# Later transposes and attention pairs, pooling sums on VectorE, and features-first values in a one-core decoder layer

## The chip, the cores and the metric

The kernel runs on one NeuronCore of a Trainium2 chip. The metric is the device time of one launch in microseconds (us). Five engines work from queues of their own, each in program order: TensorE (PE, with PEld for its weight loads) multiplies matrices into PSUM; VectorE (DVE), ScalarE (ACT) and GpSimd (POOL) do elementwise work; SyncE (SP) issues the transfers. GpSimd is used here on SBUF only. Semaphores order the engines.

## The reference

One hybrid decoder layer on 256 tokens of 1024 features, all in float32:

```
proj = rmsnorm(x) @ w_in                  # q, k, v (512 each), u_pool 512, gates 2048
q, k = rotary(rmsnorm_per_head(q, k))     # 8 heads of 64
attn = causal softmax(q k^T / 8) v        # one block of 256 tokens, so plain causal attention
pool = (trailing mean over 2, 4, 8, 16 tokens - token) @ w_pool, scaled
g = sigmoid(gates + b)
x = x + (g0 * (attn @ w_branch_attn) + g1 * (pool @ w_branch_pool)) @ w_out
up = depthwise_conv3(rmsnorm(x) @ w_up);  gate, val = split(up)
out = x + (silu(gate) * val) @ w_down     # 2816 hidden features
```

With 256 tokens and blocks of 256, block selection selects nothing beyond the own block.

## The kernel before

Activations are kept features-first (128 features on partitions, 256 tokens along the free axis), except q, k and v, which are computed tokens-first, 128 tokens at a time. Precision comes from splitting: each operand of a large product is split into a rounded `high` part (ScalarE, L78) and the rest `low` (VectorE, L82 or L84), and `mm3` (L90 to L92) adds three products. Weights are streamed in chunks of 1 MB into four `raw` buffers; `ahead` splits the next piece (half a chunk, `hi_...` on ScalarE, `lo_...` on VectorE) some pieces before TensorE needs it, and the last `low` of a chunk issues the next load on SyncE's queue.

Every engine's work is in the order in which the Python program writes it; the last lines of the kernel tie each instruction to the one before it on its engine. So the order around the change is that of the code:

- `project` computes q, k, v. While k and v run, `norm_evacuate` (L281) normalises and rotates q and k, mostly on GpSimd (L294 to L305).
- `to_heads` (L308) transposes a normalised half of q or k with four TensorE transposes and copies it on ScalarE to `qT` or `kT` (L313).
- Four feature tiles of the pooling projection follow (two chunks `p`, two tiles each, 24 matmuls a tile). `pool_group` (L380) takes each tile, and sums shifted copies in 1 to 4 doubling steps on GpSimd; `pool_mean` comes two tiles later.
- Sixteen gate tiles follow (`ps_g`, 24 matmuls each). Four attention pairs (two heads each) are woven between them: `scores` (L422) at the gate tiles 0, 4, 8, 12, and then, through `later(n, ...)` and `tick`, which is called once per tile, `weigh` three tiles later (transposes of the weights), `values` one later, `heads_out` one later. At tile 10 `pool_maps` multiplies by `w_pool`.
- `branch` then computes the pooling branch (`ps_bp`, 8 tiles of 12 matmuls; `tick` at every second tile) and the attention branch (`ps_ba`), which needs the heads' outputs `ath` and `atl`. After that come the output projection and the ConvFFN, which the diff does not touch.

PSUM is shared: a pool of four banks (`bank`) serves the projections, the transposes and the values; a second pool with two buffers of two banks (`ps2`) serves scores, transposed weights and the pool maps. A tile that reuses a buffer waits for the last reader of the tile before.

Of the kernel before, what the change touches and what calls it, by code (L numbers as in the profile page):

```python
# [20 lines left out]
DH = 64  # L21
# [10 lines left out]
NEG = -1e30  # L32
# [18 lines left out]
STAGGER = 1  # L51
AHEAD = 4
FFN_AHEAD = 6
XCUTS = (1, 2, 4, 6, 8)


@with_exitstack
def hybrid_layer_kernel(ctx: ExitStack, tc: tile.TileContext, xq_d, par_d, wkv_d, wpg_d,
                        wpool_d, wba_d, wbp_d, wout_d, wup_d, wdn_d, out_d):
    nc = tc.nc  # L60
# [10 lines left out]
    tmp = mixer.enter_context(tc.tile_pool(name="tmp", bufs=2))  # L71

    def bank(name):
        return mm.tile([P, 512], F32, tag="mm", name=name)


    def high(hi, src, scale=1.0):
        nc.scalar.activation(hi, src, AF.Copy, scale=scale)  # L78

    def low(lo, hi, src, scale=None):  # L80
        if scale is None:
            nc.vector.tensor_tensor(lo, src, hi.bitcast(F32), ALU.subtract)  # L82
        else:
            nc.vector.scalar_tensor_tensor(lo, src, scale, hi.bitcast(F32), ALU.mult, ALU.subtract)  # L84
# [41 lines left out]
    for c, (name, src) in enumerate(order):  # L126
        n = CH if name == "q" else src.shape[-1]
# [31 lines left out]
    def ahead(upto=0):  # L159

        next_high()
        next_low()
        if at[1] - sum(p[0] < used[0] for p in pieces) < upto:
            next_high()
            next_low()
# [23 lines left out]
    cut = 0  # L189
    for k in XCUTS:  # L190
        end = KD + k * (S + AW)
# [9 lines left out]
    for i in range(WARM):  # L201
        nc.tensor.matmul(warm[:, 0:P], ones, ones, start=True, stop=True)

    ident = const.tile([P, P], F32, name="ident")
# [2 lines left out]
    nc.gpsimd.memset(mhalf, -0.5)  # L207
    mask = const.tile([P, 3, P], F32, name="mask")
    nc.gpsimd.memset(mask, 0.0)
    nc.gpsimd.affine_select(out=mask[:, 1:3, :], in_=mask[:, 1:3, :], compare_op=ALU.is_ge, fill=NEG,  # L210
                            base=0, pattern=[[0, 2], [-1, P]], channel_multiplier=1)
    rcnt = const.tile([P, 16], F32, name="rcnt")
    nc.gpsimd.iota(rcnt, pattern=[[1, 16]], base=1, channel_multiplier=0,
# [38 lines left out]
    qT, kT = qkT[:, 0], qkT[:, 1]  # L252
    vn = act.tile([P, 2 * NT, AW], F32, tag="v", name="vn")
# [54 lines left out]
    def to_heads(qg, t, dst, name):  # L308
        pq = bank(f"ps_t{name}{t}")
        flat = qg.rearrange("p h d -> p (h d)")  # L310
        for j in range(KA):
            nc.tensor.transpose(pq[:, j * P:(j + 1) * P], flat[:, j * P:(j + 1) * P], ident)
        nc.scalar.activation(dst[:, :, t * P:(t + 1) * P], pq.rearrange("p (j c) -> p j c", c=P), AF.Copy)  # L313
# [32 lines left out]
    qg, kg, stat = [], [], []  # L346
# [2 lines left out]
    ptv = project("v", on_v)  # L349
    for t in range(NT):  # L350
        nc.scalar.activation(vn[:, t, :], ptv[t], AF.Copy, scale=rtok1[:, t:t + 1])
    for t in range(NT):
        to_heads(qg[t], t, qT, "q")


    due = {}
    clock = [0]
# [1 line left out]
    def later(n, fn, *args):  # L359
        due.setdefault(clock[0] + n, []).append((fn, args))  # L360
# [7 lines left out]
    def feature_tile(w, c, name):  # L368
        hi, lo = w
        ps = bank(f"ps_{name}")  # L370
        for k in range(KD):
            sl = slice(k * 256 + c * P, k * 256 + (c + 1) * P)
            mm3(ps[:, 0:S], (hi[:, sl], lo[:, sl]), (xhi[:, k, :], xlo[:, k, :]), k == 0, k == KD - 1)
        return ps
# [3 lines left out]
    PAD = 16  # L378

    def pool_group(g, ps):  # L380
        w = WINDOWS[g]
        u = tmp.tile([P, PAD + S], F32, tag="pu", name=f"pu{g}")
        nc.gpsimd.memset(u[:, 0:PAD], 0.0)
        nc.vector.tensor_tensor(u[:, PAD:], ps[:, 0:S], R1, ALU.mult)
        cur, step = u, 1
        while step < w:
            nxt = tmp.tile([P, PAD + S], F32, tag=f"pw{step % 3}", bufs=2, name=f"pw{g}_{step}")
            nc.gpsimd.tensor_copy(nxt[:, 0:step], cur[:, 0:step])
            nc.gpsimd.tensor_tensor(nxt[:, step:], cur[:, step:], cur[:, 0:PAD + S - step], ALU.add)
            cur, step = nxt, 2 * step  # L390
        later(2, pool_mean, g, u, cur)

# [10 lines left out]
    for b in range(2):  # L403
        w = chunk("p")
        for c in range(2):
            ps = feature_tile(w, c, f"u{b}{c}")
            tick()
            ahead()
            pool_group(2 * b + c, ps)
    for t in range(NT):  # L410
        to_heads(kg[t], t, kT, "k")


    ath = act.tile([P, KA, S], F32R, tag="ath", name="ath")
    atl = act.tile([P, KA, S], F32R, tag="atl", name="atl")
    gates = xq[:, :, S:].rearrange("p k (i s) -> p k i s", s=S)

    def gate(n):
        return gates[:, n // 2, n % 2, :]

    def scores(hp):
        ps = ps2.tile([P, 2, 512], F32, tag="ps2", name=f"ps_s{hp}")  # L422
        for j in range(2):
            rows = slice(j * DH, (j + 1) * DH)
            nc.tensor.matmul(ps[:, j, 0:S], qT[rows, hp, P:S], kT[rows, hp, :], start=True, stop=True)
            nc.tensor.matmul(ps[:, j, S:S + P], qT[rows, hp, 0:P], kT[rows, hp, 0:P], start=True, stop=True)
        sm = tmp.tile([P, 2, 3 * P], F32, tag="big", bufs=4, name=f"sm{hp}")
        nc.vector.tensor_tensor(sm, ps[:, :, 0:3 * P],
                                mask.rearrange("p a b -> p (a b)")[:, None, :].to_broadcast([P, 2, 3 * P]), ALU.add)
        mx = tmp.tile([P, 2, 2], F32, tag="mx", name=f"mx{hp}")  # L430
        nc.vector.tensor_reduce(mx[:, 1, :], sm[:, :, 0:S], axis=AX.X, op=ALU.max)
        nc.vector.tensor_reduce(mx[:, 0, :], sm[:, :, S:3 * P], axis=AX.X, op=ALU.max)
        nc.vector.tensor_scalar(mx, mx, -(DH ** -0.5), None, op0=ALU.mult)
        sums = tmp.tile([P, 2, 2], F32, tag="sums", name=f"sums{hp}")
        for j in range(2):
            for t, cols in ((1, slice(0, S)), (0, slice(S, 3 * P))):
                nc.scalar.activation(sm[:, j, cols], sm[:, j, cols], AF.Exp, bias=mx[:, t, j:j + 1],
                                     scale=DH ** -0.5, accum_out=sums[:, t, j:j + 1])
        later(3, weigh, hp, sm, sums)

    def weigh(hp, sm, sums):
        pp = ps2.tile([P, 2, 512], F32, tag="ps2", name=f"ps_p{hp}")
        for j in range(2):
            for b in range(3):
                nc.tensor.transpose(pp[:, j, b * P:(b + 1) * P], sm[:, j, b * P:(b + 1) * P], ident)
        rs = tmp.tile([P, 2, 2], F32, tag="rs", name=f"rs{hp}")
        nc.vector.reciprocal(rs, sums)
        pT = tmp.tile([P, 2, 3 * P], F32, tag="big", bufs=4, name=f"pT{hp}")
        nc.scalar.activation(pT, pp[:, :, 0:3 * P], AF.Copy)
        later(1, values, hp, pT, rs)  # L450

    def values(hp, pT, rs):
        po = bank(f"ps_o{hp}")
        pov = po[:, 0:2 * P].rearrange("p (t j d) -> p t j d", t=2, j=2)
        for j in range(2):
            h = 2 * hp + j
            cs = slice(h * DH, (h + 1) * DH)
            nc.tensor.matmul(pov[:, 0, j, :], pT[:, j, S:3 * P], vn[:, 0, cs], start=True, stop=True)
            nc.tensor.matmul(pov[:, 1, j, :], pT[:, j, 0:P], vn[:, 0, cs], start=True, stop=False)
            nc.tensor.matmul(pov[:, 1, j, :], pT[:, j, P:S], vn[:, 1, cs], start=False, stop=True)  # L460
        an = tmp.tile([P, 2, 2, DH], F32, tag="an", name=f"an{hp}")
        nc.vector.tensor_tensor(an, pov, rs[:, :, :, None].to_broadcast([P, 2, 2, DH]), ALU.mult)
        later(1, heads_out, hp, an)

    def heads_out(hp, an):
        pa = bank(f"ps_a{hp}")
        for t in range(NT):
            nc.tensor.transpose(pa[:, t * P:(t + 1) * P], an[:, t].rearrange("p j d -> p (j d)"), ident)
        high(ath[:, hp, :], pa[:, 0:S])
        low(atl[:, hp, :], ath[:, hp, :], pa[:, 0:S])  # L470

    waiting = list(range(KD, 2 * KD)) + list(range(KD))

# [21 lines left out]
            low(pooll[:, g, :], poolh[:, g, :], o, par[:, C_PS + g:C_PS + g + 1])  # L495

    for n in range(2 * KD):
        if n % 4 == 0:
            scores(n // 4)
        if n == 10:  # L500
            pool_maps()
            ahead()
        b, c = n // 2, n % 2
        if c == 0:
            w = chunk("g")
        ps = feature_tile(w, c, f"g{n}")
        tick()
        ahead(AHEAD if n % 2 else 0)
        nc.vector.tensor_tensor(gate(n), ps[:, 0:S], R1, ALU.mult)
        if n >= 2 * KD - 2:  # L510
            sigmoids(3)
# [22 lines left out]
    tmp = ctx.enter_context(tc.tile_pool(name="ffn", bufs=2))  # L534
# [122 lines left out]
    ps = [bank("ps_up1_0")]  # L657
# [8 lines left out]
    for i in range(1, KF):  # L666
        if i > 1:
            w = chunk("up")
            ps = [up_tile(w, 0, i)]
# [8 lines left out]
        if i >= LAG:  # L678
# [92 lines left out]
```

## Time and profile before

| | |
|---|---|
| time, median of 3 runs | 358.66 us (357.54 to 359.63) |
| time of the profiled execution | 356.89 us |
| its span on the core | 355.1 us |
| mean granted TensorE clock | 0.995 |
| busy: PE, DVE, ACT, POOL | 344.3, 255.3, 195.4, 101.7 us |

The profile is of one execution. L with a number is a line of the kernel. A group's row gives line, engine, operation, output <- inputs, shapes and count, then busy time and mean, then the engine's idle time just before and what ended it. In a timeline a row starts with the start and the duration in us; several equal instructions in sequence are merged (x4). Matmuls overlap in TensorE's pipeline, so the spacing of their starts, not their duration, is what one costs. A two-pass float32 matmul is two instructions.

### The profile page before, as it was taken

The numbers are of one execution on the slowest core, as the hardware profiler recorded it, in microseconds if no ns is written. First come the engines' busy times: TensorE is split into PE (matmuls) and PEld (weight loads), VectorE is DVE, ScalarE is ACT, GpSimd is POOL, SyncE is SP. The second block draws the span as 40 slices with busy tenths as digits, with TensorE's granted clock in tenths as the row PEclk, the third lists the DMA queues.
The fourth block names the chain that finished last, engine by engine and source line by source line (L and its number), as shares of the span: only waits on it lengthen the run. The fifth ranks groups of instructions, "written<-read, shape, count | busy, mean of one in ns | idle before, by whom it ended". The sixth has DMA issues, their size and how long they took to land.

```text
span 355.1 us, 6775 instructions
## 1 busy us (share of the span) xinstructions
PE 344.3 (97%) x2760; PEld 334.5 (94%) x2760; DVE 255.3 (72%) x401; ACT 195.4 (55%) x311; POOL 101.7 (29%) x127
## 2 busy tenths in 40 slices
PE   8999895999999999999999999999999999999996
PEld 6887794999999999999999999999999999999996
DVE  4879727944677597499789986667777777777743
ACT  5955614636464984566467565555555555556420
POOL 1008999100000006379232222121212121212140
PEclk9999998999999999999999999999999999999999
DMA  7985623244263464075534764646455453642003
GB/s 281 420 341 178 252 90 119 49 173 170 116 236 120 173 258 163 6 293 194 221 117 140 278 236 180 220 145 231 134 222 185 172 228 128 238 132 107 2 0 118
DMA packets 10254, 62.76 MB, mean 177 GB/s; under 512 B 1136, under 2 KB 2288, under 8 KB 3312
## 3 DMA queue, kind: packets, MB, share of 16 engines
q1 hardware_dynamic: 10224, 62.34, 48.3%
q8 instruction: 21, 0.34, 0.4%
q14 instruction: 9, 0.07, 0.1%
HBM read 61.29 MB, written 1.05 MB: 176 GB/s over the span
## 4 chain that ended last, share of the span: by engine, by line
PE 75%; POOL 8%; DVE 8%; DMA 3%; ACT 2%; issue 2%; SPq 1%; POOLq 0%
PE ps_up L91 11%; PE ps_up L90 11%; PE ps_up L92 11%; PE ps_d L633 6%; PE ps_d L632 6%; PE ps_d L634 6%; PE ps_g L90 5%; PE ps_g L91 4%; PE ps_g L92 4%; DMA raw_k<-in_wkv 3%; DVE lo_up L82 2%; DVE hlo L84 2%; POOL rh_k L294 1%; POOL rh_q L294 1%; PE ps_bp L90 1%
## 5 line engine op out<-in xcount | busy, mean ns | idle before, releaser
L91 PE MATMUL ps_up<-hlo,hi_up 128*128 128x256 f32 x352 | 98.5, 280 | 0.2 <-DVE hlo L84 0.2
L90 PE MATMUL ps_up<-hhi,hi_up 128*128 128x256 f32 x352 | 98.7, 280 | 0.0
L92 PE MATMUL ps_up<-hhi,lo_up 128*128 128x256 f32 x352 | 98.4, 280 | 0.0
L91 PEld LDWEIGHTS ps_up<-hlo,hi_up 128*128 128x128 f32 x352 | 66.2, 188 | 0.4 <-DVE hlo L84 0.4
L90 PEld LDWEIGHTS ps_up<-hhi,hi_up 128*128 128x128 f32 x352 | 66.2, 188 | 0.0
L92 PEld LDWEIGHTS ps_up<-hhi,lo_up 128*128 128x128 f32 x352 | 66.2, 188 | 0.0
L82 DVE TENSOR_TENSOR lo_up<-raw_up,hi_up 128x1024 fp32r<-128x1024 f32 x44 | 55.9, 1274 | 6.1 <-ACT hi_up L78 6.1
L615 POOL TENSOR_TENSOR c_v<-c_g,c_v 128x256 f32<-128x256 f32 x22 | 16.3, 740 | 120.7 <-DVE c_v L598 120.7
L633 PE MATMUL ps_d<-al,hi_dn 128*128 128x256 f32 x176 | 49.2, 280 | 0.0
L634 PE MATMUL ps_d<-ah,lo_dn 128*128 128x256 f32 x176 | 49.2, 280 | 0.0
L632 PE MATMUL ps_d<-ah,hi_dn 128*128 128x256 f32 x176 | 49.2, 279 | 0.0
L78 ACT ACTIVATE hi_up<-raw_up 128x1024 fp32r<-128x1024 f32 x44 | 44.9, 1045 | 0.0
L90 PE MATMUL ps_g<-xhi,hi_g 128*128 128x256 f32 x128 | 37.5, 293 | 0.0
L91 PE MATMUL ps_g<-xlo,hi_g 128*128 128x256 f32 x128 | 36.3, 284 | 0.0
L92 PE MATMUL ps_g<-xhi,lo_g 128*128 128x256 f32 x128 | 36.3, 284 | 0.0
L78 ACT ACTIVATE ah<-c_v 128x256 fp32r<-128x256 f32 x22 | 9.2, 418 | 45.9 <-POOL c_v L615 45.9
L634 PEld LDWEIGHTS ps_d<-ah,lo_dn 128*128 128x128 f32 x176 | 33.1, 188 | 0.0
L632 PEld LDWEIGHTS ps_d<-ah,hi_dn 128*128 128x128 f32 x176 | 33.1, 188 | 0.0
L633 PEld LDWEIGHTS ps_d<-al,hi_dn 128*128 128x128 f32 x176 | 33.1, 188 | 0.0
L545 POOL TENSOR_TENSOR xq<-xq 128x256 f32<-128x256 f32 x8 | 7.0, 887 | 74.1 <-issue 70.1
L82 DVE TENSOR_TENSOR lo_dn<-raw_dn,hi_dn 128x1024 fp32r<-128x1024 f32 x22 | 27.8, 1265 | 0.4 <-ACT hi_dn L78 0.4
L603 DVE TENSOR_TENSOR u_v<-ps_up,R 128x256 f32<-128x256 f32 x22 | 9.3, 422 | 26.1 <-PE ps_up L92 26.1
(191 smaller groups left out, 843.7 us busy)
## 6 DMA issues: line engine op xcount, KB each, us to landing
raw_up<-in_wup SPq DMA_DIRECT2D x22, 1024.0 KB, 4.8
raw_dn<-in_wdn SPq DMA_DIRECT2D x11, 1024.0 KB, 4.8
raw_g<-in_wpg SPq DMA_DIRECT2D x8, 1024.0 KB, 4.8
raw_o<-in_wout SPq DMA_DIRECT2D x4, 1024.0 KB, 4.8
xq<-in_xq SPq DMA_DIRECT2D x3, 768.0 KB, 7.3
raw_v<-in_wkv SPq DMA_DIRECT2D x2, 1024.0 KB, 14.0
raw_p<-in_wpg SPq DMA_DIRECT2D x2, 1024.0 KB, 6.3
raw_bp<-in_wbp SPq DMA_DIRECT2D x2, 1024.0 KB, 5.5
```

Of the source, the lines that this page charges most:

```text
L78: nc.scalar.activation(hi, src, AF.Copy, scale=scale)
L82: nc.vector.tensor_tensor(lo, src, hi.bitcast(F32), ALU.subtract)
L84: nc.vector.scalar_tensor_tensor(lo, src, scale, hi.bitcast(F32), ALU.mult, ALU.subtract)
L90: nc.tensor.matmul(out, sh, mh, start=start, stop=False, **kw)
L91: nc.tensor.matmul(out, sh, ml, start=False, stop=False, **kw)
L92: nc.tensor.matmul(out, sl, mh, start=False, stop=stop, **kw)
L294: nc.gpsimd.tensor_tensor(rh, ss, mhalf[:, 0:H], ALU.pow)
L603: nc.vector.tensor_tensor(u, ps[:, 0:S], R2, ALU.mult)
L615: nc.gpsimd.tensor_tensor(uc[1], g[1], uc[1], ALU.mult)
L632: nc.tensor.matmul(o, hi[:, sl], acch[i], start=first, stop=False, skip_group_check=True)
L633: nc.tensor.matmul(o, hi[:, sl], accl[i], start=False, stop=False, skip_group_check=True)
L634: nc.tensor.matmul(o, lo[:, sl], acch[i], start=False, stop=i == KF - 1, skip_group_check=True)
```

## The change

1. `to_heads` for q moves from before the pooling tiles to after the first two of them; `to_heads` for k moves from after the pooling tiles to just before gate tile 1 (`KREADY`).
2. `scores` runs at gate tiles 2, 6, 10, 14 (`FIRST`) instead of 0, 4, 8, 12, and `weigh` four tiles after it instead of three.
3. The doubling sums of `pool_group` run on VectorE, and without the copies of the first columns: each step starts at column 2·step − 1, since only columns from 16 − w on are ever read. The memset of the padding moves to VectorE as well.
4. The softmax weights are divided by their sums before they are transposed: the reciprocal directly follows the exponentials, and two GpSimd products per pair multiply the weights. `values` then multiplies with v as the stationary operand, so that the output is features-first; each head writes one half of the partitions. The division after the values, the two transposes and `heads_out` go; `high` and `low` read the values' PSUM bank directly.
5. The three 128-column blocks of a pair's scores are reordered (tokens 0 to 127 first), and the mask with them.

```diff
+KREADY = 1
+FIRST = 2
...
-    nc.gpsimd.affine_select(out=mask[:, 1:3, :], in_=mask[:, 1:3, :], compare_op=ALU.is_ge, fill=NEG,
+    nc.gpsimd.affine_select(out=mask[:, 0:3:2, :], in_=mask[:, 0:3:2, :], compare_op=ALU.is_ge, fill=NEG,
...
-    for t in range(NT):
-        to_heads(qg[t], t, qT, "q")
...
-        nc.gpsimd.memset(u[:, 0:PAD], 0.0)
+        nc.vector.memset(u[:, 0:PAD], 0.0)
...
-            nc.gpsimd.tensor_copy(nxt[:, 0:step], cur[:, 0:step])
-            nc.gpsimd.tensor_tensor(nxt[:, step:], cur[:, step:], cur[:, 0:PAD + S - step], ALU.add)
+            a = 2 * step - 1
+            nc.vector.tensor_tensor(nxt[:, a:], cur[:, a:], cur[:, a - step:PAD + S - step], ALU.add)
...
             pool_group(2 * b + c, ps)
-    for t in range(NT):
-        to_heads(kg[t], t, kT, "k")
+        if b == 0:
+            for t in range(NT):
+                to_heads(qg[t], t, qT, "q")
...
+    TOK = (slice(0, P), slice(P, 3 * P))
...
-            nc.tensor.matmul(ps[:, j, 0:S], qT[rows, hp, P:S], kT[rows, hp, :], start=True, stop=True)
-            nc.tensor.matmul(ps[:, j, S:S + P], qT[rows, hp, 0:P], kT[rows, hp, 0:P], start=True, stop=True)
+            nc.tensor.matmul(ps[:, j, P:3 * P], qT[rows, hp, P:S], kT[rows, hp, :], start=True, stop=True)
+            nc.tensor.matmul(ps[:, j, 0:P], qT[rows, hp, 0:P], kT[rows, hp, 0:P], start=True, stop=True)
...
-        later(3, weigh, hp, sm, sums)
+        rs = tmp.tile([P, 2, 2], F32, tag="rs", name=f"rs{hp}")
+        nc.vector.reciprocal(rs, sums)
+        for t in (1, 0):
+            n = TOK[t].stop - TOK[t].start
+            nc.gpsimd.tensor_tensor(sm[:, :, TOK[t]], sm[:, :, TOK[t]],
+                                    rs[:, t, :, None].to_broadcast([P, 2, n]), ALU.mult)
+        later(4, weigh, hp, sm)
...
-        later(1, values, hp, pT, rs)
-
-    def values(hp, pT, rs):
+        later(1, values, hp, pT)
+
+    def values(hp, pT):
+
         po = bank(f"ps_o{hp}")
-        pov = po[:, 0:2 * P].rearrange("p (t j d) -> p t j d", t=2, j=2)
-        for j in range(2):
-            h = 2 * hp + j
-            cs = slice(h * DH, (h + 1) * DH)
-            nc.tensor.matmul(pov[:, 0, j, :], pT[:, j, S:3 * P], vn[:, 0, cs], start=True, stop=True)
-            nc.tensor.matmul(pov[:, 1, j, :], pT[:, j, 0:P], vn[:, 0, cs], start=True, stop=False)
-            nc.tensor.matmul(pov[:, 1, j, :], pT[:, j, P:S], vn[:, 1, cs], start=False, stop=True)
-        an = tmp.tile([P, 2, 2, DH], F32, tag="an", name=f"an{hp}")
-        nc.vector.tensor_tensor(an, pov, rs[:, :, :, None].to_broadcast([P, 2, 2, DH]), ALU.mult)
-        later(1, heads_out, hp, an)
-
-    def heads_out(hp, an):
-        pa = bank(f"ps_a{hp}")
-        for t in range(NT):
-            nc.tensor.transpose(pa[:, t * P:(t + 1) * P], an[:, t].rearrange("p j d -> p (j d)"), ident)
-        high(ath[:, hp, :], pa[:, 0:S])
-        low(atl[:, hp, :], ath[:, hp, :], pa[:, 0:S])
+        for b in range(2):
+            for j in range(2):
+                h = 2 * hp + j
+                nc.tensor.matmul(po[j * DH:(j + 1) * DH, b * P:S], vn[:, b, h * DH:(h + 1) * DH],
+                                 pT[:, j, 2 * b * P:(2 * b + 2 - b) * P], start=b == 0, stop=b == 1)
+        high(ath[:, hp, :], po[:, 0:S])
+        low(atl[:, hp, :], ath[:, hp, :], po[:, 0:S])
...
     for n in range(2 * KD):
-        if n % 4 == 0:
-            scores(n // 4)
+        if n == KREADY:
+            for t in range(NT):
+                to_heads(kg[t], t, kT, "k")
+        if n >= FIRST and (n - FIRST) % 4 == 0:
+            scores((n - FIRST) // 4)
```

More of the change, by code (lines that the diff above doesn't have):

```diff
@@ L430, in scores @@
         mx = tmp.tile([P, 2, 2], F32, tag="mx", name=f"mx{hp}")
-        nc.vector.tensor_reduce(mx[:, 1, :], sm[:, :, 0:S], axis=AX.X, op=ALU.max)
-        nc.vector.tensor_reduce(mx[:, 0, :], sm[:, :, S:3 * P], axis=AX.X, op=ALU.max)
+        for t in (1, 0):
+            nc.vector.tensor_reduce(mx[:, t, :], sm[:, :, TOK[t]], axis=AX.X, op=ALU.max)
         nc.vector.tensor_scalar(mx, mx, -(DH ** -0.5), None, op0=ALU.mult)
@@ L435, in scores, with weigh @@
         for j in range(2):
-            for t, cols in ((1, slice(0, S)), (0, slice(S, 3 * P))):
-                nc.scalar.activation(sm[:, j, cols], sm[:, j, cols], AF.Exp, bias=mx[:, t, j:j + 1],
+            for t in (1, 0):
+                nc.scalar.activation(sm[:, j, TOK[t]], sm[:, j, TOK[t]], AF.Exp, bias=mx[:, t, j:j + 1],
                                      scale=DH ** -0.5, accum_out=sums[:, t, j:j + 1])
-        later(3, weigh, hp, sm, sums)
-    def weigh(hp, sm, sums):
+        rs = tmp.tile([P, 2, 2], F32, tag="rs", name=f"rs{hp}")
+        nc.vector.reciprocal(rs, sums)
+        for t in (1, 0):
+            n = TOK[t].stop - TOK[t].start
+            nc.gpsimd.tensor_tensor(sm[:, :, TOK[t]], sm[:, :, TOK[t]],
+                                    rs[:, t, :, None].to_broadcast([P, 2, n]), ALU.mult)
+        later(4, weigh, hp, sm)
+    def weigh(hp, sm):
         pp = ps2.tile([P, 2, 512], F32, tag="ps2", name=f"ps_p{hp}")
@@ L445, in weigh @@
                 nc.tensor.transpose(pp[:, j, b * P:(b + 1) * P], sm[:, j, b * P:(b + 1) * P], ident)
-        rs = tmp.tile([P, 2, 2], F32, tag="rs", name=f"rs{hp}")
-        nc.vector.reciprocal(rs, sums)
         pT = tmp.tile([P, 2, 3 * P], F32, tag="big", bufs=4, name=f"pT{hp}")
         nc.scalar.activation(pT, pp[:, :, 0:3 * P], AF.Copy)
-        later(1, values, hp, pT, rs)
-    def values(hp, pT, rs):
+        later(1, values, hp, pT)
+    def values(hp, pT):
         po = bank(f"ps_o{hp}")
-        pov = po[:, 0:2 * P].rearrange("p (t j d) -> p t j d", t=2, j=2)
-        for j in range(2):
-            h = 2 * hp + j
-            cs = slice(h * DH, (h + 1) * DH)
-            nc.tensor.matmul(pov[:, 0, j, :], pT[:, j, S:3 * P], vn[:, 0, cs], start=True, stop=True)
-            nc.tensor.matmul(pov[:, 1, j, :], pT[:, j, 0:P], vn[:, 0, cs], start=True, stop=False)
-            nc.tensor.matmul(pov[:, 1, j, :], pT[:, j, P:S], vn[:, 1, cs], start=False, stop=True)
-        an = tmp.tile([P, 2, 2, DH], F32, tag="an", name=f"an{hp}")
-        nc.vector.tensor_tensor(an, pov, rs[:, :, :, None].to_broadcast([P, 2, 2, DH]), ALU.mult)
-        later(1, heads_out, hp, an)
-    def heads_out(hp, an):
-        pa = bank(f"ps_a{hp}")
-        for t in range(NT):
-            nc.tensor.transpose(pa[:, t * P:(t + 1) * P], an[:, t].rearrange("p j d -> p (j d)"), ident)
-        high(ath[:, hp, :], pa[:, 0:S])
-        low(atl[:, hp, :], ath[:, hp, :], pa[:, 0:S])
+        for b in range(2):
[5 more added lines that the diff above has]
+        low(atl[:, hp, :], ath[:, hp, :], po[:, 0:S])
     waiting = list(range(KD, 2 * KD)) + list(range(KD))
```

## The prediction

> **What bounds the kernel now.** I read the page's head, then TensorE's waits, the chain of waits, the timeline around the longest wait, and the stage tables.
>
> ```profile
> span 355.1 us, 6775 instructions
> ...
> PE 344.3 (97%) x2760; PEld 334.5 (94%) x2760; DVE 255.3 (72%) x401; ACT 195.4 (55%) x311; POOL 101.7 (29%) x127
> ```
>
> TensorE is busy nearly throughout, so only two things can help: filling its holes, or giving it less to do. Its waits, longest first (total, times, longest):
>
> ```profile
> PE ps_s L425 <- ACT qkT L313: 4.1, 1, 4.1
> ...
> PE ps_tq L312 <- POOL qg_q L305: 1.0, 1, 1.0
> ```
>
> The two waits with attention's names are what the change aims at. The chain of waits (start, duration, what) shows what lies behind the long one:
>
> ```profile
> 51.64 0.47 POOL qg_k L305
> 52.41 0.59 POOL pw L389
> ...
> 56.45 0.56 DVE pl L399
> 57.45 0.95 ACT hi_g L78
> 58.40 0.98 ACT qkT L313 x2
> 59.42 0.73 PE ps_s L425 x4
> ```
>
> GpSimd ends the normalisation of k at 52.1, only then starts the pooling sums, VectorE waits for these sums, ScalarE for VectorE, and the copies of kᵀ (L313) stand behind all that on ScalarE's queue. TensorE's timeline (in brackets the idle time before):
>
> ```profile
> 40.85 0.60 PE L312 MATMUL ps_tq<-ident,qg_q 128*128 128x128 f32 x4
> 42.42 0.66 PE L312 MATMUL ps_tq<-ident,qg_q 128*128 128x128 f32 x4 [0.97 <-POOL qg_q L305]
> 42.84 0.37 PE L90 MATMUL ps_u<-xhi,hi_p 128*128 128x256 f32 x1
> ...
> 54.24 1.03 PE L312 MATMUL ps_tk<-ident,qg_k 128*128 128x128 f32 x8
> 59.42 0.73 PE L425 MATMUL ps_s<-qkT 64*128 64x256 f32 x4 [4.15 <-ACT qkT L313]
> ...
> 61.31 0.42 PE L90 MATMUL ps_g<-xhi,hi_g 128*128 128x256 f32 x1
> 61.52 0.41 PE L91 MATMUL ps_g<-xlo,hi_g 128*128 128x256 f32 x1
> ```
>
> Between 42.84 and 54.24 lie 96 matmuls, one every 0.119 us; after the hole one starts every 0.21 us. The stage table (PE, PEld, DVE, ACT, POOL busy, then clock, DMA) shows why:
>
> ```profile
> 55.27:59.42 4.15, 0.00 (x2) 0.01 (x1) 3.16 (x7) 2.57 (x5) 3.96 (x9) 1.00 0.71 253
> 59.42:64.00 4.58, 4.58 (x26) 4.33 (x27) 3.27 (x8) 0.55 (x3) 3.65 (x10) 0.63 0.01 2
> 60.00:120.00 60.00, 60.00 (x506) 59.12 (x503) 39.23 (x72) 31.71 (x66) 3.14 (x8) 0.97 0.41 145
> ```
>
> After the hole the granted clock is 0.63 over 4.58 us, that is half speed for 3.4 us. From 60 to 120, TensorE never idles and VectorE has 20.8 us to spare.
>
> **The change, part by part.**
>
> *Holes (removed).* The q transposes go behind the first two pooling tiles, the k transposes behind the first gate tile, the first scores behind the second. A tile of 24 matmuls takes 24 x 0.119 = 2.85 us. So from the end of v at 40.85: tiles to 46.6, q transposes (8 x 0.12) to 47.6, tiles to 53.3, first gate tile to 56.1, k transposes to 57.1, second gate tile to 60.0. GpSimd has q at 42.4 and k at 52.1: 4 us of margin for both. Removed: 0.97 + 4.15, and with them the slow clock: 3.4 us in which a matmul took 0.21 instead of 0.12, 1.5 us. **Minus 6.6.** That lies on the bounding engine, ahead of the 295 us from 60 on, so all of it counts. The next thing late is the copies of kᵀ, needed at 60.0.
>
> *Pooling sums on VectorE.* Ten additions over some 270 columns and four memsets; the ten copies vanish, since each addition starts at the column where the previous sum is valid. No VectorE row has this shape; the nearest adds two SBUF tiles of 256:
>
> ```profile
> L82 DVE TENSOR_TENSOR pooll<-pl,poolh x4: 394/414/422, 56.9 to 69.4; 128x256 fp32r<-128x256 f32 x4
> ```
>
> 10 x 0.42 + 4 x 0.1 = 4.6 us between 44 and 57. Until now VectorE waited for GpSimd there:
>
> ```profile
> 45.95 0.42 DVE L384 TENSOR_TENSOR pu<-ps_u,R 128x256 f32<-128x256 f32 x1 [3.90 <-PE ps_u L92]
> ...
> 53.03 0.43 DVE L396 SCALAR_TENSOR_TENSOR pl<-pw,pu 128x256 f32<-128x256 f32 x1 [3.83 <-POOL pw L389]
> ```
>
> These 7.7 us of idling cover the 4.6. VectorE's groups from 60 to 120 (busy, mean ns, idle before) give the `lo` that queues there, and two waits for later:
>
> ```profile
> L82 DVE TENSOR_TENSOR lo_g<-raw_g,hi_g 128x1024 fp32r<-128x1024 f32 x13 | 15.8, 1218 | 0.0
> ...
> L462 DVE TENSOR_TENSOR an<-ps_o,rs 128x256 f32<-128x256 f32 x4 | 1.7, 424 | 10.6 <-PE ps_o L460 10.6
> ...
> L82 DVE TENSOR_TENSOR atl<-ps_a,ath 128x256 fp32r<-128x256 f32 x3 | 1.3, 425 | 6.7 <-ACT ath L78 6.7
> ```
>
> Played forward in program order (a `lo` 1.2, each group's means 0.43 and two short ones, 0.75), VectorE has the third group's means at about 57.1, and ScalarE behind them the high part 0.4, one `hi` 0.95 and two copies 0.98 (both in the chain above): kᵀ at 59.5 against 60.0. Half a microsecond is thin, and GpSimd still runs k's chain beside it. I charge **0.4**, with 0 and 2 as ends (2 is when every addition is stretched by half; without the cover all 4.6 would count). GpSimd's rows for the next sentences and the next part:
>
> ```profile
> 49.41 1.04 POOL L295 TENSOR_TENSOR qg_k<-qg_k,rh_k 128x512 f32<-128x512 f32 x1
> ...
> 57.35 1.62 POOL L389 TENSOR_TENSOR pw<-pw 128x270 f32<-128x270 f32 x1
> ...
> 59.17 0.63 POOL L389 TENSOR_TENSOR pw<-pw 128x268 f32<-128x268 f32 x1
> ```
>
> The Trainium skill speaks against this part: SBUF — State Buffer (its section on engine ports) says that a VectorE instruction with two SBUF inputs and a GpSimd instruction that reads SBUF lock each other out for a whole instruction. The trace agrees: the GpSimd addition L389 took 1.62 us beside a `lo` and 0.63 alone. By the rule alone, ten additions push k's chain back by 4.2 us, from 52.1 to 56.3, and the k transposes at 56.1 wait 0.2: inside my ends.
>
> *Values features-first.* Six matmuls of two passes, the division on VectorE, two transposes and their dependencies go; four matmuls of two passes come, which move 256 or 128 columns and write 64 partitions each, the two heads alternating. The old cost, and the nearest row to the new one, stand side by side:
>
> ```profile
> 73.77 0.33 PE L458 MATMUL ps_o<-vn,pT 128*128 128x64 f32 x2
> ...
> 74.83 0.39 PE L460 MATMUL ps_o<-vn,pT 128*128 128x64 f32 x2
> 75.14 0.71 PE L425 MATMUL ps_s<-qkT 64*128 64x256 f32 x4
> 75.68 0.40 PE L426 MATMUL ps_s<-qkT 64*128 64x128 f32 x4
> 76.00 0.38 PE L90 MATMUL ps_g<-xhi,hi_g 128*128 128x256 f32 x1
> ```
>
> Old: 12 passes from 73.77 to 75.05 (one every 0.11), 1.28 us; the two transposes 0.22 (the k transposes: 1.03 for 8, less the last one's tail). The scores are also four two-pass matmuls of 256 and 128 columns in two half-arrays, and take from 75.05 to 76.00, 0.95 us with both changes of shape. Only they split the rows, the new ones the columns; no run of before splits columns. Taken as the scores: 4 x (1.50 - 0.95) = **minus 2.2**. Ends: heads that don't overlap at all, 1.7 us a pair, and loads unhidden on top (8 x 0.1), 2.5 us: plus 4.0 in all; best, without the changes of shape (0.75), minus 3.0. I take the scores' row as the nearest because it matches in columns, passes and alternation.
>
> *Division on GpSimd, and later ticks.* Per pair one 128x512 and one 128x256 product; the broadcast product L295 took 1.04 us, so 1.7 with the smaller at 0.63, as L389. GpSimd is busy for 3.14 of the 60 us from 60 to 120. The weighing waits four tiles instead of three, 11.4 us after the scores; mask, maxima, exponentials and division need some 2.2 + 1.9 + 1.7, which leaves 5.6 for queueing. Nothing. The reciprocal, though, now stands on VectorE right behind the maxima and waits out the exponentials:
>
> ```profile
> 79.35 0.51 ACT L437 ACTIVATE sm<-sm,mx 128x256 f32<-128x256 f32 x1 [5.42 <-DVE mx L433]
> ...
> 81.03 0.19 ACT L437 ACTIVATION_READ_ACCUMULATOR sm<-sm,mx 128x1 f32 x1
> ```
>
> 1.9 us a pair, with the `lo` pieces queued behind it. Its cover is VectorE's idling of 10.6 us for the values, which goes with `an`; without it 7.6 us would have to come out of the rest of the 20.8.
>
> *Two tighter places.* The pool maps at the tenth tile now follow one pair's transposes and the next one's scores directly, and take the PSUM buffer that the 0.81 us copy `pT` frees: 1.0 against 0.95 of scores: **0.2** (to 1). The last pair's values come at the sixth of eight `bp` tiles instead of before the first, so that ScalarE, with the exponentials now moved up against its sigmoids, reaches `ath` late:
>
> ```profile
> 115.88 0.81 ACT L449 ACTIVATE pT<-ps_p 128x768 f32<-128x768 f32 x1 [1.76 <-PE ps_p L445]
> ...
> 128.63 0.90 ACT L477 ACTIVATE xq<-xq,par 128x256 f32<-128x256 f32 x2
> 129.43 2.00 ACT L78 ACTIVATE hi_o<-raw_o 128x1024 fp32r<-128x1024 f32 x2
> ```
>
> ScalarE works without a break from 115.9 to 131.4, and `ath` would follow the last sigmoids, 2 us before the `ba` tiles begin. On VectorE, `atl`, a `lo` and a product stand between it and the release of a PSUM bank: 0.4 + 1.2 + 0.4. I charge **0.6** (0 to 2). Loads keep their place relative to the tiles; the weights arrive no later against TensorE.
>
> Sum: -6.6 - 2.2 + 0.4 + 0.2 + 0.6 = **-7.6 us**. The profiled execution took 356.89 us, so 349.3 for its like; it lies 1.8 us under the median 358.66, which gives **351.1**. A measurement can tell about 0.5%, 1.8 us.
>
> **The rivals.**
>
> *Columns don't overlap.* For it: no row shows the form. Against it: the half-arrays of the scores overlap. Heads in turn, 1.7 us a pair: +0.8 instead of -2.2, 354.1; with unhidden loads +4.0, 357.3.
>
> *The hole comes back at the first scores.* For it: the 0.5 us of margin, and GpSimd beside VectorE's additions. Against it: GpSimd's sums, the longest link of the chain, are gone. With kᵀ 3 us late, +2.6: 353.7; over 3.4 us the slow clock returns too, +1.5 more: about 356.
>
> *VectorE becomes the bound, slower than before.* The place is the attention stage: 39.2 busy, less 1.7 for `an`, plus 7.6 of waiting for exponentials, 6.8 if the divisions lock it out, the remaining waits for `atl` (6.7) and 4.6 of pooling backlog: 63.2 against about 56 us of TensorE work, 7.2 late. If TensorE then starves once a pair for over 3.4 us, four slow clocks add 6.0: -8.8 + 13.2 = +4.4, 363.1. It decides once VectorE lags by more than the four `hi`/`lo` pieces of lead, some 11 us. Against it: waits for `atl` are idling while ahead, and shrink first.
>
> **How the numbers follow.** Forecast 0.60; columns in turn 0.19 (of that 0.04 near 357); hole back 0.12; VectorE bound 0.04; more than forecast (all ends good: -6.6 - 3.0 = -9.6, 349, and 1.2 of run spread) 0.05. The forecast's own range is 349 to 353. The range 347.5 to 355.5 takes in the first two rivals' main cases and leaves out the unhidden loads and the slow case. Faster by over 0.5% (under 356.9): 0.60 + 0.15 + 0.11 + 0.05, some 0.90; within: 0.06; slower: 0.04.
>
> **What would show it.** TensorE without a wait over 1 us between 40 and 62, and a clock of 1.00 there (holes); the values' slot near 0.95 us and no `ps_a` transposes; `pw` rows on VectorE of 0.4 us; gaps under 1 us before `ps_m` and the first `ps_ba`. Wrong would be a wait of 3 us or more on `ps_s`, values rows of 1.7 us a pair, or TensorE waiting for `lo_g`.

## The result, and the profile after

| | before | after |
|---|---|---|
| median | 358.57 us (357.54 to 359.63, 4 runs) | 348.68 us (348.67 to 348.89, 4 runs) |
| profiled execution | 356.89 us | 348.69 us |
| its span | 355.1 us | 346.9 us |

The ratio is 0.9729, 95% interval 0.9703 to 0.9755: 2.7% faster. The forecast was 351.1 us with a range of 347.5 to 355.5. Between the two profiled executions the gain is 8.2 us against a forecast of 7.6; between the medians it is 9.9. The further 1.7 us belong to the runs of the kernel before, which differ from one another by up to 3 us for two reasons that the last section tells (two paces of TensorE, and a slow clock of two lengths). Four runs of 482 to 1926 us, in a slow state, two of them of the kernel before, are left out here and below.

TensorE's waits after, from its view of waits (total, times, longest):

```profile
PE ps_warm L204 <- DVE ones L178: 1.0, 1, 1.0
PE ps_s L430 <- ACT qkT L315: 0.5, 1, 0.5
```

The 4.1 us for kᵀ have become 0.5, the 1.0 us for q is gone. TensorE's timeline after, around the first scores (start, duration, idle before in brackets):

```profile
46.67 1.03 PE L314 MATMUL ps_tq<-ident,qg_q 128*128 128x128 f32 x8
...
55.96 1.04 PE L314 MATMUL ps_tk<-ident,qg_k 128*128 128x128 f32 x8
...
59.52 0.27 PE L94 MATMUL ps_g<-xhi,lo_g 128*128 128x256 f32 x1
60.27 0.71 PE L430 MATMUL ps_s<-qkT 64*128 64x256 f32 x4 [0.47 <-ACT qkT L315]
60.80 0.40 PE L431 MATMUL ps_s<-qkT 64*128 64x128 f32 x4
61.35 0.28 PE L93 MATMUL ps_g<-xlo,hi_g 128*128 128x256 f32 x1
61.46 0.28 PE L94 MATMUL ps_g<-xhi,lo_g 128*128 128x256 f32 x1
```

Both transposes run without a wait, the scores come 0.5 us late, and behind them a matmul starts every 0.12 us at once: no slow clock. The stage table says the same of the clock, in its third column from the right:

```profile
41.06:61.20 20.14, 19.67 (x170) 19.31 (x168) 17.53 (x40) 10.19 (x16) 11.71 (x14) 1.00 0.43 163
60.00:120.00 60.00, 59.63 (x508) 56.82 (x508) 44.30 (x70) 38.75 (x80) 9.69 (x8) 1.00 0.48 173
```

VectorE is at 17.5 of 20.1 us between 41 and 61 and at 44.3 of 60 in the attention stage, so it did not become the bound. VectorE's rows (start, duration) give the first group's one addition, then two rows that the working below needs, the fourth group's four additions in a row, and behind these the third group's means:

```profile
44.53 1.08 DVE L389 TENSOR_TENSOR pw<-pu 128x271 f32<-128x271 f32 x1
...
50.55 0.42 DVE L383 TENSOR_TENSOR pu<-ps_u,R 128x256 f32<-128x256 f32 x1 [0.34 <-PE ps_u L94]
...
52.93 0.41 DVE L398 TENSOR_TENSOR fix<-pw,rcnt 128x3 f32<-128x3 f32 x1
...
55.39 0.44 DVE L389 TENSOR_TENSOR pw<-pu 128x271 f32<-128x271 f32 x1
55.87 1.37 DVE L389 TENSOR_TENSOR pw<-pw 128x269 f32<-128x269 f32 x3
57.15 0.42 DVE L396 SCALAR_TENSOR_TENSOR pl<-pw,pu 128x256 f32<-128x256 f32 x1
57.49 0.15 DVE L398 TENSOR_TENSOR fix<-pw,rcnt 128x7 f32<-128x7 f32 x1
57.68 0.17 DVE L399 TENSOR_TENSOR pl<-fix,pu 128x7 f32<-128x7 f32 x1
```

The third group's means are there at 57.85 (forecast 57.1). ScalarE's rows after give the rest of that chain:

```profile
57.88 0.42 ACT L80 ACTIVATE poolh<-pl 128x256 fp32r<-128x256 f32 x1 [2.94 <-DVE pl L399]
58.20 1.05 ACT L80 ACTIVATE hi_g<-raw_g 128x1024 fp32r<-128x1024 f32 x1
59.15 1.06 ACT L315 ACTIVATE qkT<-ps_tk 128x512 f32<-128x512 f32 x2
```

kᵀ is complete at 60.2 instead of the forecast 59.5, and was wanted at 59.8. And the new values, from the timeline of one pair:

```profile
76.84 0.28 PE L94 MATMUL ps_g<-xhi,lo_g 128*128 128x256 f32 x1
77.05 0.87 PE L467 MATMUL ps_o<-pT,vn 128*64 128x256 f32 x8
77.85 0.39 PE L92 MATMUL ps_g<-xhi,hi_g 128*128 128x256 f32 x1
78.07 0.28 PE L93 MATMUL ps_g<-xlo,hi_g 128*128 128x256 f32 x1
```

The slot runs from 76.96, where the next matmul would have started, to 77.85: 0.89 us (forecast 0.95). The matmul behind it is followed after 0.22 us instead of 0.12, so another 0.1 belongs to the slot: 1.0 us in place of 1.28 + 0.22, where the 0.22 has the way out in it.

### The profile page after: what moved, and what is told of

Same layout as the page of the kernel before. It is cut to its first block, busy times and chain, and to the rows that moved or that the text cites. A ratio compares the mean times of both kernels' runs of the same rounds, so it can differ in the third digit from the quotient of the medians.

```text
span 346.9 us, 6715 instructions
## 1 busy us (share of the span) xinstructions
PE 340.7 (98%) x2736; PEld 329.2 (95%) x2736; DVE 261.0 (75%) x411; ACT 195.7 (56%) x311; POOL 101.5 (29%) x111
## 4 chain that ended last, share of the span: by engine, by line
PE 80%; DVE 10%; DMA 4%; ACT 2%; issue 2%; SPq 1%; POOL 0%; ACTq 0%
PE ps_up L93 11%; PE ps_up L94 11%; PE ps_up L92 11%; PE ps_d L636 6%; PE ps_d L637 6%; PE ps_d L635 6%; PE ps_g L92 4%; PE ps_g L94 4%; PE ps_g L93 4%; DMA raw_k<-in_wkv 4%; PE ps_v L278 3%; DVE lo_up L84 2%; DVE hlo L86 2%; PE ps_bp L92 1%; PE ps_ba L94 1%
## 5 line engine op out<-in xcount | busy, mean ns | idle before, releaser
L92 PE MATMUL ps_g<-xhi,hi_g 128*128 128x256 f32 x128 | 36.5, 285 | 0.0
L642 POOL TENSOR_TENSOR al<-c_v,ah 128x256 fp32r<-128x256 f32 x22 | 23.0, 1045 | 11.6 <-ACT ah L80 11.6
```

What stands on the lines that cost most here:

```text
L92: nc.tensor.matmul(out, sh, mh, start=start, stop=False, **kw)
L642: nc.gpsimd.tensor_tensor(accl[i], act_i, acch[i].bitcast(F32), ALU.subtract)
```

## The experiments

For orientation, the fastest runs of each kernel, which the last section makes comparable: before 356.9, after 348.6.

**1. The later places alone.** Before, with the moves of `to_heads` and `scores`; sums on GpSimd, old values.

```diff
-    for t in range(NT):
-        to_heads(qg[t], t, qT, "q")
...
+        if b == 0:
+            for t in range(NT):
+                to_heads(qg[t], t, qT, "q")
...
-        if n % 4 == 0:
-            scores(n // 4)
+        if n == 1:
+            for t in range(NT):
+                to_heads(kg[t], t, kT, "k")
+        if n >= 2 and (n - 2) % 4 == 0:
+            scores((n - 2) // 4)
```

> Before with the later places of transposes and scores alone; the sums stay on GpSimd and the values as they were. My theory (the chain through GpSimd's sums makes the hole): the copies of k still stand behind the third group's means, which GpSimd's sums give at about 60.6, so k is there at 63 instead of 60.0, a wait of about 3 us stays at the first scores: 353.5 to 355.1 us, 1.5 more if the clock falls. Rival (the order alone fills the hole, where the sums run is indifferent): 350.9 us and no wait over 0.5 us.

Measured: 354.86 us median (fastest 354.55), ratio 0.9916 (0.9883 to 0.9949). TensorE still waits around the first scores, in two places now:

```profile
PE ps_s L424 <- ACT qkT L313: 1.4, 1, 1.4
PE ps_g L90 <- DVE pu L382: 1.3, 1, 1.3
...
PE ps_g L92 <- DVE lo_g L82: 0.4, 1, 0.4
```

3.1 us in all, with kᵀ at 63.3 (forecast 63):

```profile
63.34 0.71 PE L424 MATMUL ps_s<-qkT 64*128 64x256 f32 x4 [1.39 <-ACT qkT L313]
```

The order alone brings 2.3 of the 8.3 us between the fastest runs. The second wait was not foreseen: VectorE, which had idled 5.8 us for GpSimd (the end of k's chain, then the sums) before 53.0, released a PSUM bank late. The clock stayed at 1.00 behind both waits.

**2. The later places and the sums on VectorE**, old values.

```diff
-            nc.gpsimd.tensor_copy(nxt[:, 0:step], cur[:, 0:step])
-            nc.gpsimd.tensor_tensor(nxt[:, step:], cur[:, step:], cur[:, 0:PAD + S - step], ALU.add)
+            a = 2 * step - 1
+            nc.vector.tensor_tensor(nxt[:, a:], cur[:, a:], cur[:, a - step:PAD + S - step], ALU.add)
```

(on top of the first experiment's diff, with the memset)

> Before with the later places and the sums on VectorE; the values and the division as they were. My theory (the values are worth 2.2 us): 348.7 + 2.2 = 350.9 us. Rival (the medians fell by 9.9, the profiled executions by 8.2; the rest belongs to the values, worth 3.9): 352.6 us. Rival (the values are worth nothing, the holes everything): 348.7 us.

Measured: 352.24 us median, runs at 351.4 and 353.1, ratio 0.9836 (0.9790 to 0.9882). The median points to the rival (352.6), but the runs lie at two levels 1.7 us apart, and the changed kernel has the same two (experiment 12). Level for level, 351.4 against 348.7: the values are worth 2.7 us in this surrounding. Of that 4 x (1.50 - 1.0) = 2.0 is the slot and 0.3 a wait of the old form (the second row below). The remaining 0.4 stands in the output projection, whose matmuls take 22.83 us in this trace and 22.40 in that of the changed kernel; nothing shows that the values' form is the cause. The waits of this run:

```profile
PE ps_s L424 <- ACT qkT L313: 0.4, 1, 0.4
PE ps_o L457 <- ACT pT L448: 0.3, 1, 0.3
```

**3. The sums on VectorE alone**: only the second experiment's diff, transposes, scores and values as before.

> Before with the sums on VectorE alone; transposes, scores and values where they were. My theory: k's copies no longer wait for GpSimd's sums and follow the k transposes at about 56.4, a wait of 1.2 us instead of 4.15 and no slow clock, the wait for q (1.0) stays: 352.6 to 354.2 us. Rival (the wait comes from the scores standing right behind the transposes, so the sums' engine is indifferent): 358.6 us.

Measured: 354.55 us median (fastest 353.59), ratio 0.9919 (0.9889 to 0.9950). TensorE's timeline:

```profile
54.06 1.03 PE L312 MATMUL ps_tk<-ident,qg_k 128*128 128x128 f32 x8
57.56 0.71 PE L425 MATMUL ps_s<-qkT 64*128 64x256 f32 x4 [2.47 <-ACT qkT L313]
```

The wait falls from 4.15 to 2.5 us (forecast 1.2: the copies began, and did not end, at 56.4). The clock stays at 1.00 in the profiled execution, but not in all: six of the ten runs have a mean granted clock of 0.998 or more, the other four 0.990 to 0.995, at 355.2 to 356.9 us. So the slow clock still comes in part of the runs, which I had not expected, though no trace shows one of them. Each of the two parts shortens the same hole, and neither closes it: in the fastest runs the order brings 2.3 us, the sums 3.3, and both together 5.5.

**4. The values alone.** Before, with the diff's new `values` and the division before the transposes, the transposes three tiles after the scores as before.

```diff
+        rs = tmp.tile([P, 2, 2], F32, tag="rs", name=f"rs{hp}")
+        nc.vector.reciprocal(rs, sums)
...
+            nc.gpsimd.tensor_tensor(sm[:, :, TOK[t]], sm[:, :, TOK[t]],
+                                    rs[:, t, :, None].to_broadcast([P, 2, n]), ALU.mult)
-        later(3, weigh, hp, sm, sums)
+        later(3, weigh, hp, sm)
```

> Before with features-first values and the division on GpSimd alone. My theory: four slots of 0.9 us instead of 1.5: 2.2 us less, 356.4 us, and the 4.15 us wait with its slow clock stays. Rival (worth 3.9): 354.7 us. Rival (GpSimd's divisions beside its sums delay the first pair, or the change of array shape eats the gain): 358.6 us or more.

Measured: 359.00 us median (357.38 to 360.11), ratio 1.0016 (0.9991 to 1.0041): no gain. Its waits show why:

```profile
PE ps_s L427 <- ACT qkT L313: 4.2, 1, 4.2
PE ps_p L453 <- POOL sm L445: 2.1, 2, 1.3
```

The transposes now wait 2.1 us for GpSimd's division, which three tiles do not cover, and that takes back the 2.0 of the shorter slots. The profiled execution, at 360.11 us, is the slowest of these runs. The clock behind the old hole is one reason, the slower pace of the last section another. The stage table:

```profile
59.40:64.00 4.60, 4.59 (x22) 4.21 (x23) 2.17 (x4) 0.54 (x3) 3.68 (x10) 0.50 0.01 4
64.00:70.00 6.00, 6.00 (x48) 6.00 (x48) 4.58 (x11) 2.90 (x10) 1.63 (x2) 0.89 0.04 8
```

Before had 0.63 and then 1.00 in these stretches. Here the clock was already slow at 58.4, while TensorE still waited, and stayed so until 65.3: 6.8 us, twice as long. The new form does not decide this. The mean granted clock of each run tells the two lengths apart (3.4 us at half speed in 355 make 0.995, twice that makes 0.990): of these ten runs five are at 0.994 or 0.995 and five at 0.989 or 0.990, and the kernel before has both lengths as well (last section).

**10. The values alone, transposed four tiles after the scores.**

```diff
-        later(3, weigh, hp, sm)
+        later(4, weigh, hp, sm)
```

> Before with features-first values and the division on GpSimd as in e4_values, but with the weights transposed four tiles after the scores instead of three. My theory (e4_values lost its gain to 2.1 us of waiting for the division at the transposes): no wait on ps_p, and the fastest runs at 356.9 - 2.4 = 354.5 us. Rival (the new form doesn't pay without the other parts): 356.5 us or more in the fastest runs too.

Measured: 358.03 us median (356.38 to 359.38, 12 runs), ratio 0.9990 (0.9963 to 1.0016). The wait for the division is gone, and another has come:

```profile
PE ps_s L427 <- ACT qkT L313: 4.2, 1, 4.2
...
PE ps_tq L312 <- POOL qg_q L305: 1.0, 1, 1.0
PE ps_s L427 <- ACT pT L455: 0.9, 1, 0.9
```

Transposes and the next scores now stand back to back, as in the changed kernel, and one scores wait 0.9 us for the buffer that `pT` frees. My 354.5 is refuted, but so is the rival's "doesn't pay" in its full strength. The profiled execution (359.14 us) has the longer slow clock and the slower pace of the last section, so that it can't be set beside that of before. The runs can be, clock for clock: at 0.993 to 0.995 they lie at 356.4 and at 358.0 to 358.1 us, those of before in the same comparison at 356.9 to 357.0 and at 358.6 to 358.9. So the new values gain 0.5 to 0.8 us in this surrounding, where the shorter slots alone would give 2.0. The wait takes 0.9 back. Behind the last matmul this trace needs 4.05 us instead of 3.56, and why is open.

**5. The hole filled.** Before, with work for TensorE where it waits.

```diff
+        if n == 0:
+            for i in range(32):
+                nc.tensor.matmul(stat[0][:, 1, 0:S], xhi[:, i % KD, 0:P], xhi[:, i % KD, :], start=True, stop=True)
         if n % 4 == 0:
             scores(n // 4)
```

> Before with 32 extra matmuls (results unused) between the k transposes and the first scores, where TensorE otherwise waits for 4.15 us: the wait for k stays as long, only TensorE's idling goes. My theory (the hole costs 4.15 us of waiting and 1.5 us of slow clock behind it): the clock stays at 1.00, the profiled execution falls by 1.5 to 355.4 us. If the slow stretch also makes the runs of before differ by 2 us, the runs lie within 0.3 us of each other and the median falls by 3, to about 355.4; if the spread has another source, it stays at 2 us and the median is 357.1. Rival (no slow clock cost): 358.6 us.

Measured: 356.41 us median, the profiled execution 355.44, ratio 0.9960 (0.9939 to 0.9981). TensorE's timeline and the stage table:

```profile
55.00 4.08 PE L500 MATMUL ps_n<-xhi 128*128 128x256 f32 x32
59.39 0.71 PE L425 MATMUL ps_s<-qkT 64*128 64x256 f32 x4 [0.32 <-ACT qkT L313]
59.92 0.39 PE L426 MATMUL ps_s<-qkT 64*128 64x128 f32 x4
```

```profile
59.40:64.00 4.60, 4.60 (x40) 4.45 (x41) 3.52 (x8) 1.29 (x5) 3.91 (x10) 1.00 0.02 5
```

The scores begin at 59.4 as before, the clock is 1.00 instead of 0.63, and 1.45 us are gone: that is the price of the slow clock in its shorter length, by itself, and it was forecast as 1.5. The runs are at two levels, 355.3 to 355.6 and 357.2 to 357.3, where the runs of before are spread over 356.9 to 359.9. Every one of these runs has a mean granted clock of 0.998 or more. So the slow clock made part of that spread, but a step of 1.8 us has another source. My expectation of 0.3 us of spread is refuted.

**6 and 7. Do the two halves of the array overlap?** After, with the four matmuls written head by head; and after, with both heads in one half.

```diff
-        for b in range(2):
-            for j in range(2):
+        for j in range(2):
+            for b in range(2):
```

```diff
-                nc.tensor.matmul(po[j * DH:(j + 1) * DH, b * P:S], vn[:, b, h * DH:(h + 1) * DH],
+                nc.tensor.matmul(po[0:DH, j * S + b * P:(j + 1) * S], vn[:, b, h * DH:(h + 1) * DH],
...
-        high(ath[:, hp, :], po[:, 0:S])
-        low(atl[:, hp, :], ath[:, hp, :], po[:, 0:S])
+        for j in range(2):
+            high(ath[j * DH:(j + 1) * DH, hp, :], po[0:DH, j * S:(j + 1) * S])
+        for j in range(2):
+            low(atl[j * DH:(j + 1) * DH, hp, :], ath[j * DH:(j + 1) * DH, hp, :], po[0:DH, j * S:(j + 1) * S])
```

(the second on top of the first)

> After, with the four matmuls of the values written head by head instead of alternating. My theory (the two halves of the array overlap whatever the order, as the scores do, which are written head by head): same, 348.7 us, slot 0.9 us. Rival (only the alternation makes them overlap): slot 1.6 us a pair, 351.5 us.

> After, with both heads' values computed in the same half of the array, so that they can't overlap (two half-size copies and differences instead of one follow on ScalarE and VectorE, which have spare time). My theory: slot 1.5 to 1.7 us a pair instead of 0.9, 2.4 to 3.2 us more: 351.1 to 351.9 us. Rival (the new form is short for another reason, such as shorter weight loads): 348.7 us.

Measured: head by head 349.67 us median, runs at 348.5 to 348.8 and 350.55, the fastest as after; in one half 351.46 us (351.40 to 351.61). The slots, head by head:

```profile
76.98 0.28 PE L94 MATMUL ps_g<-xhi,lo_g 128*128 128x256 f32 x1
77.19 0.88 PE L467 MATMUL ps_o<-pT,vn 128*64 128x256 f32 x8
78.00 0.39 PE L92 MATMUL ps_g<-xhi,hi_g 128*128 128x256 f32 x1
```

and in one half:

```profile
76.74 0.28 PE L94 MATMUL ps_g<-xhi,lo_g 128*128 128x256 f32 x1
76.95 1.51 PE L467 MATMUL ps_o<-pT,vn 128*64 128x256 f32 x8
78.40 0.38 PE L92 MATMUL ps_g<-xhi,hi_g 128*128 128x256 f32 x1
```

0.90 us (77.10 to 78.00) in the first, 1.54 (76.86 to 78.40) in the second; 4 x 0.65 = 2.6 of the 2.8 us between the medians 351.46 and 348.68. The overlap of the halves is the values' whole gain: without it the new form, at 1.54 and 0.1 more on the way out, is no better than the old 1.50, and the time is that of the old form (351.4 in experiment 2). It does not hang on the written order.

**8. k's transposes ahead of the means.** After, with the transposes and copies of k written before the tick that runs the third group's means.

```diff
-        if n == KREADY:
-            for t in range(NT):
-                to_heads(kg[t], t, kT, "k")
...
         ps = feature_tile(w, c, f"g{n}")
+        if n == KREADY - 1:
+            for t in range(NT):
+                to_heads(kg[t], t, kT, "k")
         tick()
```

> After, with the k transposes and copies written ahead of the tick that holds the third group's means, so that the copies no longer stand behind them on ScalarE's queue. My theory: the 0.5 us wait left at the first scores goes, 348.2 us. Rival (means and split weights behind the copies then come late instead): 348.7 us or more.

Measured: 348.11 us (348.00 to 348.12), ratio to before 0.9734 (0.9713 to 0.9755); the changed kernel's fastest run is 348.6. ScalarE's rows:

```profile
56.41 1.08 ACT L315 ACTIVATE qkT<-ps_tk 128x512 f32<-128x512 f32 x2 [1.65 <-PE ps_tk L314]
57.70 0.42 ACT L80 ACTIVATE poolh<-pl 128x256 fp32r<-128x256 f32 x1 [0.20 <-DVE pl L399]
```

kᵀ is there at 57.5, 2 us before it is wanted, and the wait is gone. This kernel is 0.6 us faster than the changed one, about the size of that wait.

**9. The division on VectorE.** After, with `nc.vector` for `nc.gpsimd` in the two products.

> After, with the division of the weights on VectorE instead of GpSimd. My theory (VectorE has idle time in the attention stage, the engine of the division is off the path): 4 x 1.7 us more on VectorE and no change within 0.3 us, 348.7 us. Rival (VectorE is near its limit there, so GpSimd's taking the division is part of the gain): weights split late, waits on lo_g, 350 us or more. Rival (GpSimd's divisions hold up VectorE's splits, one of which took 2.06 us beside them instead of 1.21, and that costs time): faster, 348.2 us.

Measured: 348.86 us median (fastest 348.63): no change. The engine of the division is off the path. GpSimd's products do hold VectorE up; here are VectorE's rows of the changed kernel beside a division that began at 67.69, and later:

```profile
67.78 2.06 DVE L84 TENSOR_TENSOR lo_g<-raw_g,hi_g 128x1024 fp32r<-128x1024 f32 x1
...
71.65 1.21 DVE L84 TENSOR_TENSOR lo_g<-raw_g,hi_g 128x1024 fp32r<-128x1024 f32 x1
```

but TensorE's waits after name no `lo_g`, so these 0.85 us are off the path, and with the division on VectorE itself the kernel is as fast.

**11 and 12. The two levels.** The kernel of experiment 8 with one small extra matmul in the middle of the ConvFFN, and the changed kernel once more.

```diff
+        if i == 11:
+            nc.tensor.matmul(bank("ps_break")[:, 0:P], ones, ones, start=True, stop=True)
         if i > 1:
             w = chunk("up")
             ps = [up_tile(w, 0, i)]
```

> The kernel of e8_k_first with one small extra float32 matmul (result unused) in the middle of the ConvFFN, at the eleventh pair of tiles. The traces show matmuls of 256 columns starting either every 116.7 or every 117.8 ns, the same over a whole unbroken stretch; over the ConvFFN's 1584 matmuls that is 1.75 us. My theory (the pace is drawn anew whenever the stream is interrupted): runs at three levels, about 348.3, 349.2 and 350.0 us, and both paces in some trace on the two sides of the break. Rival (drawn once per launch or before the ConvFFN): two levels, 348.3 and 350.0 us.

> The changed kernel itself, unaltered, for comparison on this chip: 348.7 us; 350.4 us in runs in which the ConvFFN's matmuls take the slower pace.

Measured: with the break 349.43 us (five runs at 349.2 to 349.5, one at 349.91); the changed kernel again at two levels, 348.6 to 348.7 and 350.5 to 350.8, ratio 0.9746 (0.9708 to 0.9785). The profiled execution with the break (349.91) has the slower pace on both sides of it, 117.78 ns. The five runs lie near the middle level of my theory and at neither level of the rival, but no trace shows both paces, so that what a break does to the pace stays open. The extra matmul itself costs little: from its first matmul to the end the ConvFFN takes 192.1 us in this trace and 192.0 at the same pace in that of experiment 6.

## Why the prediction was right, point by point

*Holes, -6.6.* Right in mechanism and in size. TensorE's idling of 0.97 + 4.15 is gone and 0.47 has come in its place; the slow clock, 1.5 by my reading of the spacing, is 1.45 by experiment 5. A further 0.4 was not priced: with matmuls right behind them the eight q transposes take 0.79 us instead of 1.02 without the wait, the k transposes 0.79 instead of 1.03, of which 0.1 is lost again on the way out. Experiments 1 and 3 show that both parts are needed to close the hole. GpSimd's chain was the cause: kᵀ came at 63.3 with the order alone, at 57.5 with the sums alone.

*The thin margin, 0.4.* Measured 0.47. Its working was less good than its result, and that the two agree is partly luck: it had kᵀ in time at 59.5 and charged 0.4 for the risk, while the means came at 57.85 instead of 57.1. The addition that GpSimd's chain stretched to 1.08 us is not why, for VectorE idled again (0.34 us) before the third tile's row at 50.55. From there it ran without a break, and beside the end of k's chain three instructions took longer than their like: the addition at 51.49 0.58 us instead of 0.44, the second group's means at 52.46 0.54 instead of 0.42, and the row at 52.93 0.41 instead of 0.15. That is 0.5 of the 0.75 us; the prediction doesn't list its steps, so the rest can't be placed. The rule of the Trainium skill that I set against this part (SBUF — State Buffer, section SBUF: two separate sides: a VectorE instruction with two SBUF inputs and a GpSimd instruction that reads SBUF lock each other out for a whole instruction) agrees with these stretched rows. My sum from it was wrong: GpSimd finished k at 53.3 instead of 52.1, 1.2 us late where I made it 4.2. Four of the ten additions came after that (from 55.39 on), and of the other six three took 0.44 us, as long as those four, and three took 1.08, 0.58 and 0.58.

*Values, -2.2.* Measured -2.0: 1.0 us a slot with the way out, instead of 1.50. The scores were the right row to take, 0.95 against 0.89, but it was misread: the 0.95 has only one of the two changes of shape in it, since the matmul at 76.00 is followed after 0.23 us instead of 0.12. The row is this one:

```profile
76.23 0.28 PE L91 MATMUL ps_g<-xlo,hi_g 128*128 128x256 f32 x1
```

Read whole, the scores would have given -1.8. Experiment 7 shows that had the halves not overlapped, the part would have brought nothing; that rival, priced at 354.1 with my 1.7 us a pair, would have come out at 351.5.

*Division and later ticks, nothing.* Right in the whole change, and experiment 9 shows it. But "nothing" hangs on the surroundings: with three tiles the transposes wait 2.1 us, and with four, in the old order, the next scores wait 0.9 (experiments 4 and 10).

*Tighter places, 0.2 and 0.6.* The pool maps cost 0.3 (the scores in front of them took 1.03 us, the other pairs' 0.86; the maps 1.52, before 1.40). The `ba` tiles cost nothing: `atl` came at 122.1, the first `ba` matmul at 123.06. I had let a bank wait for the product behind `atl`; no such wait is in TensorE's view. This term was too large by 0.6. As measured, the terms are -6.6 - 0.4 - 2.0 + 0.5 + 0.3 = -8.2, which is the gain between the profiled executions; the forecast of -7.6 lacked the shorter transposes and had the 0.6 too much, and the smaller errors (values 0.2 too large, the margin and the maps 0.1 too small each) happen to go the other way.

*From the profiled execution to the median.* Here the working failed in a way that the range hid: I carried the 1.8 us between them over to the new kernel as if they belonged to the kernel. They are the slower pace of the ConvFFN and the slow clock's length, which differ from run to run, as the last section shows; the slow clock went with the hole, the four runs after all had the faster pace, and experiment 12 shows that not all do. Of the 2.4 us between the forecast 351.1 and the measured 348.7 this step is 1.8, and the terms are 0.6. Like for like (fastest runs 356.9 and 348.6) the change is worth 8.3 us.

*Rivals.* The hole did not come back, VectorE did not become the bound (44.3 of 60 us). In the view of waits the reciprocal's wait for the exponentials is 8.0 us in all, as priced (7.6), and the wait for `atl` shrank, as argued. No run shows the 3.4 us of waiting that I took as the condition for a slow clock: in experiment 4 it came 3.2 us after TensorE ran dry (58.4 against 55.2), and in experiment 3, with 2.5 us of waiting in its trace, in four runs of ten.

## What to carry to other kernels

Ask of a hole on the bounding engine which queue each link of its chain stands in: here a copy waited on ScalarE only because unrelated work was written ahead of it, and moving that copy brought the last half microsecond for free. Two parts that shorten the same hole can add up in the fastest runs (2.3 + 3.3 against 5.5) and still leave a wait each, so look at every run's clock and not at one trace. And a part that gains 2 us in one order of the work can bring a third of that in another.

## What the runs showed of the hardware that I had not expected

TensorE has two paces at full clock. The stage table of two executions between 210 and 250 us, first of the changed kernel (348.69 us), then of experiment 6 (350.55 us), columns PE busy with the count of matmuls, granted clock, DMA:

```profile
210.00:250.00 40.00, 40.00 (x345) 1.00 0.56 196
```

```profile
210.00:250.00 40.00, 40.00 (x342) 1.00 0.53 188
```

Both are busy throughout at a clock of 1.00, yet one starts a 256-column matmul every 116.67 ns, the other every 117.78 (averages of 60 starts). Over the ConvFFN's 1584 matmuls that is 1.76 us, the step between the levels of experiments 2, 5, 6 and 12. Of the fourteen traces, four have the slower pace there, those of experiments 4, 6, 10 and 11, and each is of a run at the upper level of its kernel; the other ten are of runs at the lower one. Within one execution the pace changed only where the stream was interrupted by transposes, scores, values or a wait: in the changed kernel's profile it is slow from 88.4 to 93.6 and fast before and after. What chooses it stays open.

The slow clock after an idle stretch came in whole lengths: 3.4 us in the profile of before, 6.8 us in those of experiments 4 and 10, after the same 4.2 us of waiting. In the first it fell at 60.0, after the scores had begun; in the other two at 58.4 and 58.5, with TensorE still idle. Which length comes differs from run to run of one kernel: of 54 runs of before that stand beside the experiments, 24 have a mean granted clock of 0.993 to 0.995, at 356.9 to 357.2 and 358.6 to 358.9 us, and 30 one of 0.988 to 0.990, at 357.4 to 358.5 and 359.1 to 360.1. Two lengths and two paces thus make four levels, and they account for the spread of the runs of before. And the halves of the array overlap for two-pass float32 matmuls split by columns: 0.89 us against 1.54 for the same eight passes in one half. The scores, with the same passes and columns but split by rows, take 0.95.
